# The last up pair of a ConvFFN in seven products, and the first operands of its down stage on freed bytes

## The chip, the cores and the metric

The kernel runs on one core of one Trainium2 chip. The metric is the device time of one execution in microseconds. A core has TensorE for matrix products (PE in the profile), VectorE (DVE), ScalarE (ACT), GpSimd (POOL) and SyncE (SP), which only issues DMA transfers. Each engine has an instruction queue of its own, which it works off in order; engines wait for each other by semaphores.

## The reference

One layer of a streaming encoder on 1024 positions and 16 meta tokens, with 1024 channels. The change concerns its last part, a gated feed-forward block with a causal convolution of width 3, and a residual:

```python
def _conv_ffn(xn, w_up, conv_w, conv_b, w_down):
    seq_len = xn.shape[1]
    hid = xn @ w_up
    hp = jnp.pad(hid, ((0, 0), (CONV_WIDTH - 1, 0), (0, 0)))
    conv = conv_b + sum(hp[:, j:j + seq_len] * conv_w[j] for j in range(CONV_WIDTH))
    val, gate = jnp.split(conv, 2, axis=-1)
    return (jax.nn.silu(gate) * val) @ w_down
```

`hid` has 2 × 2816 columns, so there are 22 tiles of 128 gate columns and 22 of value columns. Behind the block stands a final RMS norm.

## The kernel before

**Precision.** Every float32 product is made of three TensorE products. An operand x is cast to a shorter form (hi, by ScalarE: "cast") and the rest x − hi is kept as lo (by VectorE or GpSimd: "split", `split_lo`, L137). Then hi·hi, hi·lo and lo·hi are added up in PSUM.

**Up.** Pair c is one tile of gate columns and one of value columns. Pairs 1, 2 and 21 are "plain" (`plain_steps`, L1338): 2 tiles × 3 pieces of about 343 positions × 8 steps over the channels × 3 = 144 matmuls, each piece followed by ScalarE (L1361, bias and first convolution weight) and two VectorE steps (L1363). Pairs 3 to 20 are "block pairs" (`block_pair`, L1486): gate and value, two halves of the channels and two halves of the positions make a 2 × 2 block product, which `seven` (L215) computes with seven block products instead of eight. These need sums of the weights (`combine`, L1451, GpSimd), casts (L1304) and splits of seven weight blocks, and sums of the positions (the tiles T, made once). Each of the seven products runs over 2 pieces of 258 and 256 positions, 4 steps and 3 matmuls: 168 matmuls. Evictions go to ScalarE (`S.copy`) and VectorE (`add`), and afterwards the convolution runs over whole rows of 1024 (L1501, L1503).

`glue` (L1311) ends both kinds: silu on ScalarE, the product with the value half (on GpSimd; on VectorE for pair 21), and the store to the scratch tensor `a_d` in DRAM (by SyncE; by ScalarE's queue for pair 21, L1320). For the pairs in `SUMMED` GpSimd makes four sums more, which are stored too.

**Down.** The 11 double tiles j of `a_d` are multiplied with `w_down`, again by seven products for a 2 × 2 block. They go in four groups, (8, 9), (7, 0, 1), (2, 3, 4), (5, 6, 10), and for each group the products p run in the order 0, 4, 1, 2, 5, 3, 6. I write (g, p) for product p of group g. `forms(p, j)` (L1561) loads a tile of weights (`wr`) and one of `a_d` (`ar`), makes the sums (GpSimd, L1570 to L1576), casts both (ScalarE, L1583) and splits both: on GpSimd for products 0, 4 and 5, on VectorE for the others. `product` (L1677 and on) runs, for four row tiles and every j of the group, three matmuls of 512 columns (L1697 to L1699); group 0 has 24 matmuls in a product, the others 36. It evicts by ScalarE (L1702, L1705) or adds on VectorE (L1707) into `u2` (four tiles, u20 to u23 in the program) and into the rows of the result, `hs`.

**What sets the order.** Operands lie in slots of four tiles (`ops`); a product's slots come free when its matmuls are done. `prepare` calls `forms` for as many products ahead as there are free slots. A scheduler then orders each engine's queue, and calls of `after(a, b)` add edges by hand. Before the change the first down operands lie in memory that is free once the tiles T are closed (`st_t.close()`), that is, once pair 20 has ended; pair 21 doesn't use T.

## Time and profile before

| | |
|---|---|
| median of 3 runs | 1427.16 us (1426.06 to 1427.6) |
| profiled execution | 1427.24 us |
| its span, from first to last instruction | 1425.5 us |
| mean granted TensorE clock | 0.998 |
| busy: TensorE, VectorE, GpSimd, ScalarE | 99%, 75%, 54%, 50% |

The profile shows one execution. A row of its timeline gives the start in us from the span's start, the duration in us, the engine, the line of the kernel, the operation, out<-in by the program's names, the shape, and in brackets how long the engine had waited and for whom. A row of a group gives the busy time of all, the mean of one in ns, and the idle time ahead of them with its releaser. A row of windows gives busy us and the number of instructions of each engine in a stretch of time, then the granted clock, the share of time that the DMA engines were busy, and GB/s.

### The profile page before, as it was taken

The numbers are of one execution on the slowest core, as the hardware profiler recorded it, in microseconds if no ns is written. First come the engines' busy times: TensorE is split into PE (matmuls) and PEld (weight loads), VectorE is DVE, ScalarE is ACT, GpSimd is POOL, SyncE is SP. The second block draws the span as 40 slices with busy tenths as digits, with TensorE's granted clock in tenths as the row PEclk, the third lists the DMA queues.
The fourth block names the chain that finished last, engine by engine and source line by source line (L and its number), as shares of the span: only waits on it lengthen the run. The fifth ranks groups of instructions, "written<-read, shape, count | busy, mean of one in ns | idle before, by whom it ended". The sixth has DMA issues, their size and how long they took to land.

```text
span 1425.5 us, 26319 instructions
## 1 busy us (share of the span) xinstructions
PE 1410.6 (99%) x9607; PEld 1336.1 (94%) x9607; DVE 1070.3 (75%) x2048; ACT 709.0 (50%) x1381; POOL 764.2 (54%) x872
## 2 busy tenths in 40 slices
PE   8999999999999999999999999999999999999997
PEld 8999999988999999999889999999999999888886
DVE  7999889843667675655479977788886776788867
ACT  7647575423555555534546444344444345644444
POOL 1542257642466556326771334545555545888795
PEclk9999999999999999999999999999999999999999
DMA  8685644530156531087953246666753327864443
GB/s 298 176 203 147 160 106 133 172 119 31 53 156 161 127 111 57 23 287 267 216 161 124 73 114 183 183 173 177 178 142 113 98 79 258 327 205 133 129 94 118
DMA packets 93318, 216.17 MB, mean 152 GB/s; under 512 B 14802, under 2 KB 22610, under 8 KB 92804
## 3 DMA queue, kind: packets, MB, share of 16 engines
q1 hardware_dynamic: 74340, 170.28, 36.3%
q0 software_dynamic: 17696, 41.29, 15.1%
q10 hardware_dynamic: 1152, 2.91, 0.7%
q8 instruction: 76, 1.25, 0.4%
q14 instruction: 54, 0.44, 0.1%
HBM read 170.88 MB, written 71.71 MB: 170 GB/s over the span
## 4 chain that ended last, share of the span: by engine, by line
PE 95%; DMA 2%; issue 1%; ACT 1%; DVE 0%; POOL 0%; POOLq 0%; DVEq 0%; SPq 0%
PE mm L174 5%; PE mm L176 5%; PE mm L175 5%; PE sp L236 4%; PE sp L237 4%; PE sp L238 4%; PE tp L236 3%; PE tp L237 3%; PE tp L238 3%; PE mm L238 3%; PE mm L236 3%; PE mm L237 3%; PE po L966 3%; PE tp L920 2%; PE mm L1699 2%; PE mm L1698 2%
## 5 line engine op out<-in xcount | busy, mean ns | idle before, releaser
L174 PE MATMUL mm<-xhi,whi 128*128 128x342 f32 (+2 forms) x480 | 156.1, 325 | 0.0
L175 PE MATMUL mm<-xlo,whi 128*128 128x342 f32 (+2 forms) x480 | 155.4, 324 | 0.0
L176 PE MATMUL mm<-xhi,wlo 128*128 128x342 f32 (+2 forms) x480 | 154.6, 322 | 0.5 <-DMA wlo<-in_w_g_dram 0.5
L1313 POOL TENSOR_TENSOR ov<-ov,og 128x1024 f32<-128x1024 f32 x21 | 50.8, 2421 | 119.7 <-ACT og L1312 117.4
L137 DVE TENSOR_TENSOR sw<-sf,sw 128x512 fp32r<-128x512 f32 x72 | 73.4, 1020 | 46.2 <-ACT sw L1304 45.1
L1304 ACT CAST sw<-sf 128x512 fp32r<-128x512 f32 x72 | 44.9, 624 | 108.9 <-POOL sf L1451 80.1
L176 PEld LDWEIGHTS mm<-xhi,wlo 128*128 128x128 f32 x480 | 90.4, 188 | 1.3 <-DMA wlo<-in_w_g_dram 0.8
L174 PEld LDWEIGHTS mm<-xhi,whi 128*128 128x128 f32 x480 | 90.4, 188 | 1.1 <-issue 0.6
L175 PEld LDWEIGHTS mm<-xlo,whi 128*128 128x128 f32 x480 | 90.4, 188 | 0.4
L1451 POOL TENSOR_TENSOR sf<-raw,sf 128x512 f32<-128x512 f32 x36 | 62.9, 1748 | 38.8 <-DVE sw L137 38.7
L1451 POOL TENSOR_TENSOR sf<-raw 128x512 f32<-128x512 f32 x36 | 49.1, 1363 | 60.0 <-ACT ov L1361 21.5
L238 PE MATMUL mm<-xhi,sw 128*128 128x258 f32 (+1 forms) x288 | 81.0, 281 | 0.0
L236 PE MATMUL mm<-xhi,sw 128*128 128x258 f32 (+1 forms) x288 | 80.8, 280 | 0.0
L237 PE MATMUL mm<-xlo,sw 128*128 128x258 f32 (+1 forms) x288 | 80.7, 280 | 0.0
L883 ACT ACTIVATE pt<-pt,mx 128x400 f32<-128x400 f32 (+5 forms) x72 | 53.1, 737 | 45.2 <-DVE mx L876 44.9
L1503 DVE SCALAR_TENSOR_TENSOR ov<-hv,cwt,ov 128x1024 f32<-128x1024 f32 x36 | 69.9, 1942 | 0.4 <-ACT ov L1501 0.4
L885 POOL TENSOR_SCALAR pt<-pt,mx 128x400 f32<-128x400 f32 (+5 forms) x72 | 51.8, 721 | 33.3 <-DVE mx L884 28.3
L1304 ACT CAST sw<-raw 128x512 fp32r<-128x512 f32 x70 | 43.0, 621 | 45.0 <-PE sp L238 23.1
L137 DVE TENSOR_TENSOR sw<-raw,sw 128x512 fp32r<-128x512 f32 x70 | 57.9, 831 | 4.3 <-ACT sw L1304 4.0
L137 DVE TENSOR_TENSOR tl<-tp,th 128x512 fp32r<-128x512 f32 (+1 forms) x80 | 50.7, 634 | 12.2 <-ACT th L923 11.6
L923 ACT CAST th<-tp 128x512 fp32r<-128x512 f32 (+1 forms) x80 | 43.4, 543 | 32.1 <-PE tp L920 22.7
L852 POOL CAST qz<-q 64x128 fp32r<-64x128 f32 (+1 forms) x72 | 20.2, 283 | 67.2 <-PE sp L871 65.7
(722 smaller groups left out, 5727.2 us busy)
## 6 DMA issues: line engine op xcount, KB each, us to landing
raw<-in_w_up_dram SPq DMA_DIRECT2D x44, 512.0 KB, 3.7
t_d<-in_w_dn_dram POOLq DMA_DIRECT2D x44, 256.0 KB, 6.9
wr<-t_d SPq DMA_DIRECT2D x44, 256.0 KB, 3.4
ar<-a_d SPq DMA_DIRECT2D x41, 256.0 KB, 5.3
a_d<-ov SPq DMA_DIRECT2D x18, 512.0 KB, 2.6
wr<-in_w_dn_dram SPq DMA_DIRECT2D x33, 256.0 KB, 3.8
t_d<-in_w_dn_dram SPq DMA_DIRECT2D x22, 256.0 KB, 4.3
t_d<-t_d SPq DMA_DIRECT2D x22, 256.0 KB, 4.7
```

The source lines that it names most:

```text
L137: return eng.tensor_tensor(out_, src, hi.bitcast(F), ALU.subtract)
L174: yield PE.matmul(ps, whi[:, i, :], ahi[:, i], start=(i == 0), stop=False)
L175: yield PE.matmul(ps, whi[:, i, :], alo[:, i], start=False, stop=False)
L176: yield PE.matmul(ps, wlo[:, i, :], ahi[:, i], start=False, stop=(i == k - 1))
L236: PE.matmul(ps, a[0][:, i], bh, start=(i == 0 and not joins), stop=False, skip_group_check=True)
L237: PE.matmul(ps, a[0][:, i], bl, start=False, stop=False, skip_group_check=True)
L238: PE.matmul(ps, a[1][:, i], bh, start=False, stop=(i == kh - 1), skip_group_check=True)
L883: ends[:] = rd, S.activation(pt[:n, :kc], pt[:n, :kc], AF.Exp, bias=low, scale=-1.0, accum_out=nm[:n, 0:1])
L885: sc_.append(GP.tensor_scalar(pt[:n, :kc], pt[:n, :kc], nm[:n, 1:2], 1.0, ALU.mult, ALU.mult))
L1304: S.copy(hi, src)
L1451: sums.append(GP.tensor_tensor(f_, a, b, op))
L1503: V.scalar_tensor_tensor(out=o, in0=h_[:, j:SEQ + j], scalar=cwc(j, m), in1=o, op0=ALU.mult, op1=ALU.add)
```

## The change

1. Pair 21 becomes a block pair. `block_pair` now ends with the seven products, and what follows (convolution, silu, product, store) is a function of its own, `conv_pair`, which for pair 21 stands behind `product(0, 0)`.
2. The first down operands no longer wait for the end of T. New memory (`down0`) holds the first buffers for `a_d` and weights; some slots are now quarters of `xhi` and `xlo`, the positions' own operands, which come free one after another as pair 21's seven products end. The forms of (0,0), (0,4), (0,1) and (0,2) are made ahead of `product(0, 0)`.
3. The store of pair 21 to `a_d` goes from ScalarE's queue to GpSimd's.
4. Edges: casts of the first products stand ahead of the first eviction copies, the convolution of pair 21 behind those casts and splits, GpSimd's splits for (1,0) behind the splits of (0,5) and (0,3), the loads of `hs` ahead of those for (0,5).

```diff
     def glue(g_, v_, c):
-        S.activation(g_, g_, AF.Silu)
+        silu = S.activation(g_, g_, AF.Silu)
+        for cp_ in first_copy:
+            after(silu, cp_)
         (V if c == NFF - 1 else GP).tensor_tensor(v_, v_, g_, ALU.mult)
...
-        (S if c == NFF - 1 else SY).dma_start(rows, v_)
+        kept[c] = (GP if c == NFF - 1 else SY).dma_start(rows, v_)
...
+    down0 = pool(ctx, "down0", side="left")
+    for tag in ("a00", "w"):
+        down0.tile([P, 512], F, tag=tag, name="hold", bufs=2)
...
+        return hg, hv
+
+    def conv_pair(c, hg, hv, behind=()):
+        res = {}
+        halves = ((hg, NFF + c, "og"), (hv, c, "ov"))
+        for h_, m, tag in halves:
+            res[tag] = o = conv_out(m, tag)
+            act = S.activation(o, h_[:, :SEQ], AF.Identity, bias=cwc(3, m), scale=cwc(0, m))
+            if behind:
+                for hi in casts[4:8]:
+                    after(act, hi)
             for j in (1, 2):
-                V.scalar_tensor_tensor(out=o, in0=h_[:, j:SEQ + j], scalar=cwc(j, m), in1=o,
-                                       op0=ALU.mult, op1=ALU.add)
-            res.append(o)
-        glue(*res, c)
+                st_ = V.scalar_tensor_tensor(out=o, in0=h_[:, j:SEQ + j], scalar=cwc(j, m), in1=o,
+                                             op0=ALU.mult, op1=ALU.add)
+                for cut in behind[:4] if tag == "og" else behind:
+                    after(st_, cut)
+                if tag == "og":
+                    last_gate[:] = st_,
+        glue(res["og"], res["ov"], c)
...
     for c in range(3, NFF - 1):
-        block_pair(c)
-    st_t.close()
-    plain_pair(NFF - 1)
...
+        conv_pair(c, *block_pair(c))
...
+    def quarter(r, h_):
+        cols = slice((L - 512) * h_, (L - 512) * h_ + 512)
+        return [[t_[:, KH * r + 2 * q + w, cols] for w in range(2) for t_ in (xhi, xlo)] for q in range(2)]
+
+    ops = quarter(0, 1)
...
+            elif j in groups[1] and p == 0:
+                for cut_ in fifth + third:
+                    after(cut, cut_)
...
             if first and p == 0:
                 first_copy.append(S.copy(to, ps))
+                for hi in casts[:4 if len(first_copy) == 1 else 8]:
+                    after(first_copy[-1], hi)
...
                 first_add.append(V.tensor_tensor(to, to, ps, ALU.subtract if p in MINUS else ALU.add))
+                if first and p == 2 and t > 1:
+                    for cut in third:
+                        after(first_add[-1], cut)
+                if len(first_add) <= 4:
+                    after(first_add[-1], last_gate[0])
...
+    last_pair = block_pair(NFF - 1)
+    ready[0, 0] = [forms(0, j) for j in groups[0]]
+    st_t.close()
+    down1 = pool(ctx, "down1", side="left")
     dpool[0] = down1
-    for p in ORDER[:2]:
+    down1.tile([P, 512], F, tag="w", name="hold", bufs=6)
...
+    ops += small + quarter(0, 0) + quarter(1, 0)
+    for p in (4, 1, 2):
         ready[0, p] = [forms(p, j) for j in groups[0]]
+    after(kept[NFF - 2], first_loads[7])
+    for c in range(4):
+        h_load.append(SY.dma_start(hs[c], h_d[P * c:P * c + P]))
+        after(h_load[-1], first_loads[-1])
+    product(0, 0, ready[0, 0], True, False)
+    conv_pair(NFF - 1, *last_pair, behind=cuts)
     st_r.close()
```

What this makes of the queues is seen in the program's own order. On VectorE, before, the end of pair 21 stands directly behind its last convolution steps; `ov` is the value half, `og` the gate half:

```order
L1363 SCALAR_TENSOR_TENSOR ov_14620<-mm_14677,cwt_9030,ov_14620 128x340 [waits Activation_49]
L1363 SCALAR_TENSOR_TENSOR ov_14620<-mm_14677,cwt_9030,ov_14620 128x340 [waits DVE_49]
L1313 TENSOR_TENSOR ov_14620<-ov_14620,og_14527 128x1024 [waits DVE_49]
L1762 MEMSET eps_14756 128x1
L1707 TENSOR_TENSOR hs0_14762<-hs0_14762,mm_14792 128x512 [waits DMAHW0_49,DMAHW6_49,PE_49,Pool_49]
L1707 TENSOR_TENSOR hs1_14763<-hs1_14763,mm_14793 128x512 [waits DMAHW5_49,DMAHW7_49,DVE_49,PE_49]
```

In the changed program the same product, now L1317, stands here; the lines L1772 are additions of the down stage, into `hs` for (0,4) and into u20 and u21 for (0,2), and the last row is the first split for (0,3):

```order
L1772 TENSOR_TENSOR hs1_14777<-hs1_14777,mm_14837 128x512 [waits DMAHW2_49,PE_49]
L137 TENSOR_TENSOR xlo_98<-ar_14826,xhi_97 128x512 [waits DMAHW0_49,Activation_49]
L1518 SCALAR_TENSOR_TENSOR ov_14872<-hv_14559,cwt_9030,ov_14872 128x1024
L1772 TENSOR_TENSOR hs2_14778<-hs2_14778,mm_14838 128x512 [waits DMAHW3_49,PE_49]
L1772 TENSOR_TENSOR hs3_14779<-hs3_14779,po_14839 128x512 [waits DMAHW4_49,PE_49]
L1518 SCALAR_TENSOR_TENSOR ov_14872<-hv_14559,cwt_9030,ov_14872 128x1024 [waits DVE_49]
L1772 TENSOR_TENSOR u20_14780<-u20_14780,mm_15063 128x512 [waits PE_49]
L1772 TENSOR_TENSOR u21_14781<-u21_14781,mm_15064 128x512 [waits PE_49]
L1317 TENSOR_TENSOR ov_14872<-ov_14872,og_14868 128x1024 [waits DVE_49,Activation_49]
L137 TENSOR_TENSOR xlo_98<-ar_14945,xhi_97 128x512 [waits DMAHW2_49,Activation_49]
```

The product has moved behind all four additions of (0,4) and two of (0,2). On GpSimd, before, pair 20's product is followed by four splits of (0,5) (into `xlo`) and by the first split of (1,0):

```order
L137 TENSOR_TENSOR op3_14714<-ar_14741,op3_14714 128x512 [waits DMAHW7_49,Activation_49]
L1313 TENSOR_TENSOR ov_14511<-ov_14511,og_14507 128x1024 [waits Activation_49,Pool_49]
L137 TENSOR_TENSOR xlo_98<-ar_14870,xlo_98 128x512 [waits DMAHW1_49,PE_49,Activation_49]
L137 TENSOR_TENSOR xlo_98<-wr_14868,xlo_98 128x512 [waits DMAHW0_49,PE_49,Activation_49]
L137 TENSOR_TENSOR xlo_98<-ar_14878,xlo_98 128x512 [waits DMAHW3_49,PE_49,Activation_49]
L137 TENSOR_TENSOR xlo_98<-wr_14876,xlo_98 128x512 [waits DMAHW2_49,PE_49,Activation_49]
L137 TENSOR_TENSOR op1_14712<-ar_14916,op1_14712 128x512 [waits PE_49,DMAHW2_49,Activation_49,Pool_49]
```

In the changed program, after pair 20's product, come four splits for (0,4) (op0 and op1), the store of pair 21, four splits for (0,5) (op2 and op3), and the first split for (1,0):

```order
L1317 TENSOR_TENSOR ov_14518<-ov_14518,og_14514 128x1024 [waits DMAHW7_49,DMAHW2_49,Activation_49]
L137 TENSOR_TENSOR op0_14772<-wr_14784,op0_14772 128x512 [waits DMAHW4_49,Activation_49]
L137 TENSOR_TENSOR op0_14772<-ar_14786,op0_14772 128x512 [waits DMAHW5_49,Activation_49]
L137 TENSOR_TENSOR op1_14773<-wr_14792,op1_14773 128x512 [waits DMAHW6_49,Activation_49]
L137 TENSOR_TENSOR op1_14773<-ar_14794,op1_14773 128x512 [waits DMAHW7_49,Activation_49]
L1324 DMA a_d_81<-ov_14872 128x1024 [waits DMASW5_49,DVE_49]
L137 TENSOR_TENSOR op2_14893<-ar_14929,op2_14893 128x512 [waits DMAHW6_49,Activation_49]
L137 TENSOR_TENSOR op2_14893<-wr_14927,op2_14893 128x512 [waits DMAHW5_49,Activation_49]
L137 TENSOR_TENSOR op3_14894<-ar_14937,op3_14894 128x512 [waits PE_49,DMAHW0_49,Activation_49,Pool_49]
L137 TENSOR_TENSOR op3_14894<-wr_14935,op3_14894 128x512 [waits DMAHW7_49,Activation_49]
L137 TENSOR_TENSOR xlo_98<-wr_14991,xhi_97 128x512 [waits PE_49,DMAHW1_49,Activation_49,Pool_49]
```

The DMA row is new on this queue, and its wait on VectorE stands ahead of the splits for (0,5).

More of the change, by code (lines that the diff above doesn't have):

```diff
@@ L212, in to_feature @@
         return los
+    kept = {}
     def m_ps():
@@ L1442, in block_kernel @@
     PIECES = [(0, 258), (258, 256)]
+    down0 = pool(ctx, "down0", side="left")
+    for tag in ("a00", "w"):
+        down0.tile([P, 512], F, tag=tag, name="hold", bufs=2)
+    eps = down0.tile([P, 1], F, name="eps")
+    V.memset(eps, EPS)
     st_t = ExitStack()
     tq = pool(st_t, "tforms", side="left")
-    T = [[tq.tile([P, KH, NH], R, name=f"t{i}{w}") for w in "hl"] for i in range(4)]
+    T = {i: [tq.tile([P, KH, NH], R, name=f"t{i}{w}") for w in "hl"] for i in (1, 2, 0, 3)}
+    T = [T[i] for i in range(4)]
     sums = []
@@ L1512, in block_kernel, with weight_tile, raw_buffer, op_tiles @@
     for c in range(3, NFF - 1):
-        block_pair(c)
-    st_t.close()
-    plain_pair(NFF - 1)
-    down1 = pool(ctx, "down1", side="left")
-    small = [down1.tile([P, 4, 512], R, name=f"op{q}") for q in range(4)]
-    ops = [[t_[:, w] for w in range(4)] for t_ in small]
-    ops += featq
-    dpool = {}
+        conv_pair(c, *block_pair(c))
[3 more added lines that the diff above has]
+    ops = quarter(0, 1)
+    n_w = [0]
+    def weight_tile():
+        n_w[0] += 1
+        if n_w[0] % 8 in (1, 2):
+            return down0.tile([P, 512], F, tag="w", name="wr", bufs=2)
+        return down1.tile([P, 512], F, tag="w", name="wr", bufs=6)
+    def raw_buffer(j, tag):
+        pl = dpool[turn_of[j] % 4 // 2]
+        if pl is dpool[0] and tag == "a00":
+            pl = down0
+        return pl.tile([P, 512], F, tag=tag, name="ar", bufs=2)
+    def op_tiles(pl, q0, q1):
+        small = [pl.tile([P, 4, 512], R, name=f"op{q}") for q in range(q0, q1)]
+        return [[t_[:, w] for w in range(4)] for t_ in small]
+    dpool = {0: None}
     pairs = {}
@@ L1531, in raw_tile @@
         if (k, h_) not in pairs.setdefault(j, {}):
-            pairs[j][k, h_] = dpool[turn_of[j] % 4 // 2].tile([P, 512], F, tag=f"a{k}{h_}", name="ar", bufs=2)
+            pairs[j][k, h_] = raw_buffer(j, f"a{k}{h_}")
         return pairs[j][k, h_]
+    first_loads = []
     def behind(ld, j):
-        if h_load and j in groups[1]:
+        if h_load and len(first_loads) == 16:
             after(ld, h_load[-1])
+        if j in groups[1]:
+            after(ld, first_loads[-1])
+        if j in groups[0]:
+            after(ld, first_loads[-1] if first_loads else kept["raw"])
+            first_loads.append(ld)
     LAST = NFF // 2 - 1
@@ L1583, in forms @@
             hi = S.copy(slot[q], src)
+            if j in groups[0] and p == 0:
+                after(hi, kept["c1"])
+            elif j in groups[0]:
+                casts.append(hi)
+                if p in (3, 6):
+                    for hi_ in casts[12:16]:
+                        after(hi, hi_)
+            elif j in groups[1] and p == 0:
+                for hi_ in casts[12:20]:
+                    after(hi, hi_)
             if first_copy and j in groups[0] and p >= 5:
@@ L1588, in forms @@
                 cuts.append(cut)
+            if j in groups[0] and p == 6:
+                late_casts.append(hi)
+            elif j in groups[0] and p == 5:
+                fifth.append(cut)
+            elif j in groups[0] and p == 3:
+                third.append(cut)
+            elif j in groups[1] and p == 0:
+                for cut_ in fifth + third:
+                    after(cut, cut_)
             if first_add and eng is V and j in groups[0] and p > 2:
@@ L1593, in forms @@
         return slot
-    first_add, first_copy, cuts = [], [], []
+    first_add, cuts, late_casts, fifth, third, casts = [], [], [], [], [], []
     held = {}
@@ L1758, in block_kernel @@
     gfB = dn.tile([P, D], F, name="gfB")
-    dn.tile([P, 512], F, tag="a00", name="hold", bufs=2)
+    for tag in ("a00", "a01", "a10", "a11"):
+        dn.tile([P, 512], F, tag=tag, name="hold", bufs=2)
+    hs.update((c, dn.tile([P, D], F, name=f"hs{c}")) for c in (7, 6))
     sq = dn.tile([P, 512], BF, name="sq")
-    eps = dn.tile([P, 1], F, name="eps")
-    V.memset(eps, EPS)
-    u2 = [dn.tile([P, 512], F, name=f"u2{c}") for c in range(4)]
-    hs = [dn.tile([P, D], F, name=f"hs{c}") for c in range(4)]
-    hs += [dn.tile([P, D], F, name=f"hs{c}") for c in range(4, KD)]
-    small2 = [dn.tile([P, 4, 512], R, name=f"op{q}") for q in range(4, 6)]
-    ops += [[t_[:, w] for w in range(4)] for t_ in small2]
-    for c in range(4):
-        h_load.append(SY.dma_start(hs[c], h_d[P * c:P * c + P]))
-    for g, p in turns:
+    ops += op_tiles(dn, 2, 4) + quarter(1, 1) + op_tiles(dn, 4, 6)
+    hs.update((c, dn.tile([P, D], F, name=f"hs{c}")) for c in (4, 5))
+    cuts.clear()
+    ops += ready[0, 0]
+    for g, p in turns[1:]:
         prepare()
```

29 lines of the change are left out of this document (16 added, 13 removed).

## The prediction

> **What bounds the kernel now.** I read the page's busy shares first, then its chain of work, then windows and single rows around the place of the change.
>
> ```profile
> PE 1410.6 (99%) x9607; PEld 1336.1 (94%) x9607; DVE 1070.3 (75%) x2048; ACT 709.0 (50%) x1381; POOL 764.2 (54%) x872
> PE 95%; DMA 2%; issue 1%; ACT 1%; DVE 0%; POOL 0%; POOLq 0%; DVEq 0%; SPq 0%
> ```
>
> TensorE is busy for 99% of the span and is 95% of the chain. So only two things move the time: a change in the matmuls that TensorE must run, and a wait that it doesn't have now. The change has one of each kind, so I look at the stage by windows: the up pair 20 (a block pair), the up pair 21 (a plain pair), and three pieces of the down stage behind it.
>
> ```profile
> core 0: us, PE busy (x) PEld busy (x) DVE busy (x) ACT busy (x) POOL busy (x), PEclk, DMA share, GB/s
> 1163.97:1183.93 19.96, 19.96 (x170) 19.96 (x169) 11.85 (x19) 7.59 (x13) 6.81 (x5) 1.00 0.29 102
> 1183.93:1206.63 22.70, 22.70 (x146) 22.70 (x145) 13.91 (x19) 13.60 (x22) 15.69 (x9) 1.00 0.79 282
> 1206.63:1215.00 8.37, 8.37 (x39) 6.95 (x38) 5.31 (x9) 5.43 (x12) 0.00 (x0) 1.00 0.66 221
> 1215.00:1222.80 7.80, 7.80 (x36) 6.44 (x35) 3.04 (x5) 6.68 (x13) 5.06 (x4) 1.00 0.81 300
> 1222.80:1248.98 26.18, 26.18 (x117) 21.56 (x116) 24.71 (x28) 15.28 (x28) 25.51 (x16) 1.00 0.96 346
> ```
>
> In every one of them TensorE is busy throughout, at a granted clock of 1.00. GpSimd (POOL) changes from idle (0.00 in the third row) to full (25.51 of 26.18 us in the last): it is the second engine at the bound here, and VectorE (DVE) beside it, with 24.71, is the third. So a delay put on GpSimd's queue at the start of the down stage has no room to be made up before the next 26 us have passed.
>
> **The gain.** These rows of TensorE's timeline are the first matmul of pair 20, of pair 21 and of the down stage. I call the last D0.
>
> ```profile
> 1163.95 0.28 PE L236 MATMUL mm<-xhi,sw 128*128 128x258 f32 x1
> 1183.93 0.32 PE L1357 MATMUL mm<-xhi,sw 128*128 128x344 f32 x1
> 1206.63 0.40 PE L1697 MATMUL mm<-op 128*128 128x512 f32 x1
> ```
>
> A block pair takes 1183.93 − 1163.95 = 19.98 us for 7 products × 2 pieces × 4 × 3 = 168 matmuls (118.9 ns each), a plain pair 1206.63 − 1183.93 = 22.70 us for 144 (157.6 ns each). Pair 21 as a block pair saves **2.72 us**. Its operands need four sums more on GpSimd and seven splits instead of four.
>
> ```profile
> L1451 POOL TENSOR_TENSOR sf<-raw,sf 128x512 f32<-128x512 f32 x36 | 62.9, 1748 | 38.8 <-DVE sw L137 38.7
> L1451 POOL TENSOR_TENSOR sf<-raw 128x512 f32<-128x512 f32 x36 | 49.1, 1363 | 60.0 <-ACT ov L1361 21.5 <-DVE sw L137 19.6 <-DMA raw<-in_w_up_dram 13.1
> ```
>
> The sums are 2 × 1.75 + 2 × 1.36 = 6.2 us, made during pair 20, in whose window GpSimd had 6.81 of 19.96 us to do. I cost them at nothing; if that cover failed, each late sum would be worth up to 1.75 us.
>
> [...]
>
> **The moves that I cost at nothing.** The first down tiles now lie on bytes that are free before the last pair ends; casts, copies, conv and splits are given an order; the loads of h move ahead of those for the sixth product, called (0,5) here (group 0, product 5), and GpSimd's next splits, for (1,0), stand behind it. I followed the rows of the new order against the durations of this trace: the operands of (0,0), (0,4), (0,1) and (0,2) come ahead of their matmuls. (0,1) is the tightest.
>
> ```profile
> 1207.77 0.62 ACT L1583 CAST xhi<-ar 128x512 fp32r<-128x512 f32 x1
> 1208.29 0.62 ACT L1583 CAST xlo<-wr 128x512 fp32r<-128x512 f32 x1
> 1222.26 0.68 DVE L137 TENSOR_TENSOR xlo<-ar,xlo 128x512 fp32r<-128x512 f32 x1
> ```
>
> Its four casts, a step of 0.52 us each, now stand behind the first eviction of (0,0), from about D0 + 2.3 to 4.4, and VectorE's last split, 0.68, ends near D0 + 5.1; the first of its matmuls is number 30 of down (D0 + 6.8, at 227 ns each). That leaves some 2 us, and what is later than that adds in full. SyncE's queue is passed by the h loads and by pair 20's store; the DMA share was 0.66 to 0.81 there, so I give them nothing, and up to 1 us if they queue.
>
> **The wait that is added.** The last pair's store of a_d moves from ScalarE's queue to GpSimd's, ahead of the four splits for (0,5). GpSimd runs in order, so all behind the store waits for the product that it stores, which VectorE makes. On VectorE that product (ov·og, 1024 columns) now stands behind the second conv step and behind the adds into u20 and u21 of product (0,2).
>
> ```profile
> 1211.28 1.23 DVE L1313 TENSOR_TENSOR ov<-ov,og 128x1024 f32<-128x1024 f32 x1
> 1225.23 0.39 PE L1697 MATMUL tp<-xlo 128*128 128x512 f32 x1
> 1225.46 0.39 PE L1698 MATMUL tp<-xlo 128*128 128x512 f32 x1
> 1230.37 0.67 DVE L1707 TENSOR_TENSOR u<-u,mm 128x512 f32<-128x512 f32 x1
> 1230.97 0.67 DVE L1707 TENSOR_TENSOR hs<-hs,mm 128x512 f32<-128x512 f32 x1
> ```
>
> Before, the product began at 1211.28, D0 + 4.65. In the new order the add of u20 waits for the 83rd matmul of down and that of u21 for the 84th; these are, by number, the rows at 1225.23 and 1225.46 (D0 + 18.60 and 18.83), whatever product they belonged to before. So u20 starts at about D0 + 18.60 + 0.39 + 0.04 = 19.03, u21 0.60 later (the step between the two adds quoted), the product 0.60 after that, and it ends at 20.23 + 1.23 = D0 + 21.46. GpSimd, done with (0,4) long before, stands idle until then.
>
> Next the store's issue on GpSimd. No row of this kernel has that store there; two groups bound it.
>
> ```profile
> L511 POOL DMA_DIRECT2D g_d<-gs x21 | 11.6, 551 | 43.3 <-ACT gs L510 39.6 <-PE tp L2120 3.7
> L1709 POOL DMA_DIRECT2D hs<-h_d x4 | 4.6, 1284 | 0.0
> ```
>
> 0.55 to 1.28 us; I take the middle, 0.9, as neither is near to it in kind (one is a store, the other runs beside this stage's splits). GpSimd is free for (0,5) at **D0 + 22.36**.
>
> ```profile
> 1215.06 1.29 POOL L137 TENSOR_TENSOR xlo<-ar,xlo 128x512 fp32r<-128x512 f32 x1 [15.45 <-ACT xlo L1583]
> 1218.83 1.29 POOL L137 TENSOR_TENSOR xlo<-wr,xlo 128x512 fp32r<-128x512 f32 x1
> 1222.81 1.29 POOL L137 TENSOR_TENSOR op<-ar,op 128x512 fp32r<-128x512 f32 x1 [2.69 <-ACT op L1583]
> 1247.29 1.74 POOL L137 TENSOR_TENSOR xhi<-ar,xhi 128x512 fp32r<-128x512 f32 x1
> 1232.03 0.39 PE L1697 MATMUL po<-xhi 128*128 128x512 f32 x1
> 1255.06 0.39 PE L1697 MATMUL tp<-op 128*128 128x512 f32 x1
> ```
>
> A split takes 1.29 us while VectorE is idle and 1.74 beside its splits. Before, the four splits of (0,5) ran from 1215.06 to 1220.12, in good time. Now they end between 22.36 + 4 × 1.27 = 27.4 and 22.36 + 4 × 1.74 = D0 + 29.3; the last is wanted by matmul number 112 (counted from 0), in the old trace 1232.03 = D0 + 25.40. I take 1.45 each, for VectorE's splits of (0,3) run beside their first half: 28.2, a **stall of 2.8 us** (2.0 to 3.9).
>
> Behind them come the 16 instructions that GpSimd had from 1222.81 to 1249.03, again as 16: twelve splits for (1,0) and (1,4) and four sums. The last belongs to (1,4) and is wanted by matmul 213, 1255.06 = D0 + 48.43 by the old trace. Before they took 25.51 us busy, 1.59 each, beside the same VectorE work; so they end at 28.2 + 25.5 = D0 + 53.7, 5.2 us late. The 2.8 us stall is part of that, not beside it: TensorE is by then 2.8 late itself, and waits 2.4 more. At 1.27 each all 20 end at 22.36 + 25.4 = D0 + 47.8, no second stall; at 1.74 each at D0 + 57.2, 8.7 late.
>
> Behind (1,4) GpSimd's next operands lay 8 us and more ahead of their matmuls by my walk through the old trace, and TensorE has itself become later by then; I give them nothing. The end of the kernel, after these, shifts with TensorE.
>
> **The sum**, against the profiled execution, 1427.24 us: −2.72 + 5.2 = +2.5, **1429.7 us**. The median of the runs shown is 1427.16, 0.08 below it, which is left as it is.
>
> **Rivals.**
> *The gain stays whole.* The store doesn't hold what stands behind it, or the change's order isn't the one that decides there. 1427.24 − 2.72 = 1424.5. For it: the four splits were done at 1220.12 and wanted no sooner than the row below, 4.4 us later. Against it: GpSimd's queue runs in its order in every stretch read. Chance 0.09; it ends near the lower edge of what counts as no change, so about half of it is faster.
>
> ```profile
> 1224.55 0.39 PE L1698 MATMUL sp<-xlo 128*128 128x512 f32 x1
> ```
>
> *Only (0,5) stalls.* GpSimd works at 1.3 us an instruction because VectorE, too, waits for the stalled TensorE. Stall 1.7 to 3.3, time 1426.2 to 1427.8. Against it is the mean of 1.59 above. Chance 0.18.
> *GpSimd and VectorE slow each other more: slower.* All 20 instructions at 1.74, and the store at 1.28: D0 + 21.46 + 1.28 + 34.8 = 57.5, 9.1 late, 1433.6. It decides for "slower" from a mean of 1.58 on, with 0.9 for the store: 22.36 + 20 × 1.58 = 54.0, 5.5 late, 1430.0. From 1247.29 on the old trace does run at 1.74, which speaks for it; the mean over the 26 us speaks against. Chance 0.15 above 1431.
> *They take turns.* [...] Chance 0.04. [...]
> *Another wait ahead of (0,5)*, at (0,1) for instance, 1 to 3 us on top: 1431 to 1433. Chance 0.04.
> *A block pair isn't shorter*, with both stalls: 1427.24 + 5.2 = 1432.4. Against it are the two windows above. Chance 0.01.
>
> **How the numbers follow.** The forecast has 0.49, spread over 1428.2 to 1431. From the median, 0.2% is 2.85 us, about what a measurement of this kernel can tell from no change: faster is under 1424.3, slower over 1430.0. The forecast splits at 1430.0 into about 0.27 same and 0.22 slower; with the rivals, slower is 0.22 + 0.15 + 0.04 + 0.04 + 0.01 = 0.46, faster 0.05, same 0.49. The range runs from 1426.0, which leaves out the whole gain, to 1433.6, GpSimd at 1.74 throughout.
>
> **What would show it.** Right: in the new profile GpSimd is idle from the end of (0,4)'s splits to about D0 + 21.5, released by VectorE's product, then issues one DMA; TensorE waits for GpSimd's splits once or twice, about 2.8 and 2.4 us, and nowhere else in the down stage; pair 21 takes 20 us. Wrong: GpSimd's splits for (0,5) begin before D0 + 15; TensorE's waits there name a DMA, ScalarE or VectorE; or a wait of more than 1 us stands ahead of (0,5) or behind (1,4).

## The result, and the profile after

The changed kernel takes **1442.85 us** (median of 4 runs, 1440.24 to 1444.65); the kernel before, in the runs beside it, 1427.38 us (1426.06 to 1427.68). The ratio is 1.0109 (95% interval 1.0088 to 1.0129): about 15 us slower, 9 us above the upper end of the predicted range, and above the time of every rival. The profiled run, 1444.55 us, is one of the two longer ones of the four (the others took 1440.24 and 1441.14).

The page of the changed kernel, its span 1442.7 us: busy time of the engines.

```profile
PE 1413.0 (98%) x9631; PEld 1335.3 (93%) x9631; DVE 1084.9 (75%) x2053; ACT 712.0 (49%) x1384; POOL 762.1 (53%) x877
```

The view of waits, TensorE's rows (us in total, times, longest). The second was there before, as 5.2; the first is new.

```profile
PE mm L1758 <- DVE xlo L137: 16.5, 1, 16.5
PE mm L357 <- ACT uh L415: 5.1, 1, 5.1
```

So one wait stands out, as long as nearly all that the span has grown by, and its releaser is VectorE, not GpSimd as forecast. Windows of pair 20, of pair 21, of the down stage up to the wait, of the wait, and of what follows:

```profile
1162.99:1182.95 19.96, 19.96 (x170) 19.96 (x169) 14.51 (x21) 8.11 (x14) 10.10 (x7) 1.00 0.23 90
1182.95:1203.00 20.05, 20.05 (x171) 20.05 (x170) 10.14 (x15) 8.29 (x15) 13.73 (x9) 1.00 0.48 153
1203.00:1225.66 22.66, 22.66 (x99) 18.16 (x98) 16.18 (x22) 18.08 (x32) 0.67 (x2) 1.00 0.81 306
1225.66:1242.13 16.47, 0.00 (x1) 0.00 (x0) 16.47 (x2) 4.56 (x8) 15.87 (x13) 0.62 0.54 176
1242.13:1245.00 2.87, 2.87 (x7) 2.29 (x8) 2.87 (x5) 0.28 (x1) 0.00 (x0) 0.50 0.61 188
```

Pair 21 takes 20.05 us. GpSimd does 0.67 us of work in the third row, as forecast. In the fourth TensorE does nothing, GpSimd works on its 13 instructions, and VectorE is "busy" for all 16.47 us with two instructions. Rows of VectorE's timeline there:

```profile
1223.45 1.22 DVE L1317 TENSOR_TENSOR ov<-ov,og 128x1024 f32<-128x1024 f32 x1
1224.59 0.68 DVE L137 TENSOR_TENSOR xlo<-ar,xhi 128x512 fp32r<-128x512 f32 x1
1225.19 16.89 DVE L137 TENSOR_TENSOR xlo<-wr,xhi 128x512 fp32r<-128x512 f32 x1
```

The product, the first split of (0,3), 0.68 us, and the second: the same instruction, 16.89 us long. GpSimd's timeline over the same time:

```profile
1224.97 0.63 POOL L1324 DMA_DIRECT2D a_d<-ov  x1 [24.00 <-DVE ov L1317]
1225.62 1.27 POOL L137 TENSOR_TENSOR op<-ar,op 128x512 fp32r<-128x512 f32 x1
...
1240.28 1.25 POOL L137 TENSOR_TENSOR op<-wr,op 128x512 fp32r<-128x512 f32 x1
```

GpSimd waited 24.00 us for the product, issued the DMA, and ran 13 instructions without a gap at 1.25 us each (beside an idle VectorE a split took 1.29 in the kernel before, at 1215.06), up to 1241.53. VectorE's split ends 0.55 us later, at 1242.08. The program orders two row tiles of (0,3) ahead of (0,5), so TensorE stands at their third matmul, which needs this split.

What TensorE did behind the wait:

```profile
1242.13 0.80 PE L1758 MATMUL mm<-xlo,xhi 128*128 128x512 f32 x1 [16.47 <-DVE xlo L137]
...
1246.57 0.43 PE L1757 MATMUL sp<-op 128*128 128x512 f32 x1
```

Ten matmuls from 1242.13 to 1246.57 take 4.44 us instead of 10 × 0.227 = 2.27, at a granted clock of 0.50 (last window above): 2.2 us more.

**The sum** of profiled spans, 1442.7 − 1425.5 = 17.2 us. The down stage begins at 1202.95 instead of D0 = 1206.63: −3.7 (0.96 of it because pair 20 starts earlier). From its first matmul to its last it takes 231.84 instead of 210.44: +21.4. Its end behind the last matmul is 0.4 shorter. Of the 21.4, 16.5 are the wait, 2.2 the half clock, and 2.7 are left. They are no wait: the 576 matmuls of down between number 312 and number 888 start here, first two rows before, last two after:

```profile
1277.51 0.39 PE L1697 MATMUL mm<-op 128*128 128x512 f32 x1
1407.87 0.27 PE L1697 MATMUL mm<-op 128*128 128x224 f32 x1
1293.56 0.40 PE L1757 MATMUL mm<-op 128*128 128x512 f32 x1
1425.49 0.27 PE L1757 MATMUL mm<-xhi 128*128 128x224 f32 x1
```

130.36 us became 131.93, 2.7 ns more for each matmul, in a stretch without a wait; over the stage's 942 matmuls that would be 2.6, as an estimate.

### The profile page after: what moved, and what is told of

Read it like the earlier page. It is cut to its first block, busy times and chain, and to the rows that moved or that the text cites. A ratio compares the mean times of both kernels' runs of the same rounds, so it can differ in the third digit from the quotient of the medians.

```text
span 1442.7 us, 26383 instructions
## 1 busy us (share of the span) xinstructions
PE 1413.0 (98%) x9631; PEld 1335.3 (93%) x9631; DVE 1084.9 (75%) x2053; ACT 712.0 (49%) x1384; POOL 762.1 (53%) x877
## 3 DMA queue, kind: packets, MB, share of 16 engines
q8 instruction: 76, 1.25, 0.4%
## 4 chain that ended last, share of the span: by engine, by line
PE 97%; DVE 2%; issue 0%; ACT 0%; DMA 0%; POOL 0%; POOLq 0%; DVEq 0%; SPq 0%
PE mm L174 6%; PE mm L175 6%; PE mm L176 5%; PE sp L238 5%; PE sp L239 5%; PE sp L240 4%; PE tp L238 3%; PE tp L239 3%; PE mm L240 3%; PE mm L238 3%; PE tp L240 3%; PE mm L239 3%; PE po L968 3%; PE tp L922 2%; PE mm L1758 2%; PE mm L1759 2%
## 5 line engine op out<-in xcount | busy, mean ns | idle before, releaser
L137 DVE TENSOR_TENSOR sw<-sf,sw 128x512 fp32r<-128x512 f32 x76 | 79.1, 1041 | 47.8 <-ACT sw L1306 47.7
L1317 POOL TENSOR_TENSOR ov<-ov,og 128x1024 f32<-128x1024 f32 x21 | 50.8, 2420 | 116.1 <-ACT og L1314 113.7
L240 PE MATMUL mm<-xhi,sw 128*128 128x256 f32 (+1 forms) x304 | 85.5, 281 | 0.0
L238 PE MATMUL mm<-xhi,sw 128*128 128x256 f32 (+1 forms) x304 | 85.3, 281 | 0.0
L239 PE MATMUL mm<-xlo,sw 128*128 128x256 f32 (+1 forms) x304 | 85.3, 280 | 0.0
L1306 ACT CAST sw<-raw 128x512 fp32r<-128x512 f32 x69 | 42.4, 621 | 43.9 <-PE sp L240 21.4
L238 PEld LDWEIGHTS mm<-xhi,sw 128*128 128x128 f32 x304 | 57.3, 188 | 0.0
```

The source lines that it names most:

```text
L137: return eng.tensor_tensor(out_, src, hi.bitcast(F), ALU.subtract)
L238: PE.matmul(ps, a[0][:, i], bh, start=(i == 0 and not joins), stop=False, skip_group_check=True)
L239: PE.matmul(ps, a[0][:, i], bl, start=False, stop=False, skip_group_check=True)
L240: PE.matmul(ps, a[1][:, i], bh, start=False, stop=(i == kh - 1), skip_group_check=True)
L1306: S.copy(hi, src)
```

## The experiments

Three questions: what holds the split; what else the change costs; and where 2.7 ns a matmul come from. E1 to e4 are edits of the changed kernel. All ratios are against the kernel before, run beside them.

### What holds VectorE's split

*Theory 1*: a run of ready instructions on GpSimd, piled up behind the late product. *Theory 2*: the DMA issue on GpSimd.

**e1**, the store on SyncE, which removes both the wait on GpSimd and the issue:

```diff
-        kept[c] = (GP if c == NFF - 1 else SY).dma_start(rows, v_)
+        kept[c] = SY.dma_start(rows, v_)
```

> Theory 1 (ready queue): in the changed kernel GpSimd, freed by the held store, ran 13 instructions with no pause, and VectorE's second split for (0,3), which reads two operands from SBUF as they do, got no turn until GpSimd paused: 16.9 us for a split of 0.68. Theory 2 (DMA issue): the store's issue on GpSimd's queue is what blocked the split that began 0.2 us behind it. Here the store goes to SyncE's queue, so neither the hold-up nor the issue is left. Both expect the wait of 16.5 us for (0,3) gone, GpSimd's splits for (0,5) at about 1215 to 1221 us, and 1424.5 to 1428.5 us: the gain of 2.7 us is kept, less up to 4 us if the loads for (1,0), which still wait for the last pair's product, come late. If something else held VectorE's split (its own operands), it stays above 1438.

1435.66 us (1434.85 to 1436.67), ratio 1.0063 (1.0051 to 1.0076). The 16.9 us split is gone, and 7.2 us with it, but the rest is far from the 1424.5 to 1428.5 that was expected. TensorE's new waits:

```profile
PE po L1757 <- DVE hs L1772: 1.9, 1, 1.9
PE mm L1758 <- DVE xlo L137: 1.8, 1, 1.8
PE tp L1757 <- DVE u L1772: 1.4, 1, 1.4
PE sp L1757 <- DVE u L1772: 0.8, 1, 0.8
```

5.9 us, all on VectorE: 1.8 for a split of (0,3), the rest for additions. The matmuls behind the first two ran at half clock, 0.43 us apart. So there is a second cost, which the long split had covered.

**e2**, the store back on ScalarE's queue:

```diff
-        kept[c] = (GP if c == NFF - 1 else SY).dma_start(rows, v_)
+        kept[c] = (S if c == NFF - 1 else SY).dma_start(rows, v_)
```

> The store goes back to ScalarE's queue, as in the kernel before. There it stands ahead of the casts for (0,5) and (0,3) and waits for VectorE's product until about 1224.6 us. Both theories expect those casts some 10 us late and a wait of TensorE for (0,3) of 3 to 6 us. Theory 1: the run of splits that GpSimd then starts takes VectorE's splits for (0,3) with it, and the wait is 10 us or more, 1435 us and above. Theory 2: no DMA issue on GpSimd, so VectorE's splits take 0.7 to 1.8 us and the time is 1427 to 1432.

1434.97 us (1434.59 to 1436.82), ratio 1.006 (1.0046 to 1.0073), between the forecasts of the two theories. No split over 1.8 us there, as theory 2 had it, and a wait of 3.2 us for ScalarE's casts, which stood behind the store. It doesn't tell e1's rest apart.

**e3**, theory 1 alone: the store on SyncE, and GpSimd's first split of (0,5) made to wait for the product:

```diff
+                if not fifth:
+                    behind_result(cut, kept["mult"])
```

> The store goes to SyncE's queue, but GpSimd's first split for (0,5) is made to wait for VectorE's product, as the store did. So the hold-up stays and the DMA issue on GpSimd goes. Theory 1: the same run without a pause, VectorE's split of 12 to 17 us, 1438 to 1445 us. Theory 2: no split above 2 us, TensorE waits under 4 us, 1426 to 1431 us.

1433.97 us (1433.83 to 1434.65), ratio 1.0052 (1.0036 to 1.0067), again between the two forecasts, with 6.2 us of waits in the down stage. GpSimd and VectorE, rows of the timeline (the first names a cast that had ended at 1215.24; VectorE's product ended at 1224.81):

```profile
1224.93 1.60 POOL L141 TENSOR_TENSOR op<-ar,op 128x512 fp32r<-128x512 f32 x1 [24.00 <-ACT op L1628]
1226.50 1.73 POOL L141 TENSOR_TENSOR op<-wr,op 128x512 fp32r<-128x512 f32 x1
1225.32 1.76 DVE L141 TENSOR_TENSOR xlo<-wr,xhi 128x512 fp32r<-128x512 f32 x1
```

The same 24.00 us of idle time, the same run, and the engines alternate, each at about 1.75 us. Theory 1 alone falls.

**e4**, theory 2 alone: the store stays on GpSimd, and the (0,5) splits wait for VectorE's last (0,3) split, so that no run stands behind the issue:

```diff
+                if len(third) == 4:
+                    for held_ in fifth:
+                        behind_result(held_, cut)
```

> The store stays on GpSimd's queue; the four splits for (0,5) behind it wait for VectorE's last split for (0,3). Theory 1: VectorE is alone for its four splits, each 0.7 us; TensorE waits under 1.5 us for (0,3) and 3 to 6 us for (0,5), and 1428 to 1434 us come out; VectorE's next splits, for (0,6), may be the ones that get no turn then. Theory 2: the split beside the DMA issue is still long, several us, and TensorE waits for it at (0,3).

1432.56 us (1432.03 to 1433.69), ratio 1.0041 (1.0028 to 1.0055), the fastest of these and within theory 1's 1428 to 1434, so that it is e3 that decides against theory 1.

```profile
1224.43 0.63 POOL L1328 DMA_DIRECT2D a_d<-ov  x1 [24.21 <-DVE ov L1321]
1224.64 0.68 DVE L141 TENSOR_TENSOR xlo<-wr,xhi 128x512 fp32r<-128x512 f32 x1
```

The split starts 0.21 us behind the start of the issue (in the changed kernel 0.22) and takes 0.68; GpSimd's first split begins only at 1226.62. Theory 2 alone falls too. *Theory 3* is left: the issue and a run of GpSimd directly behind it.

**m1**, a bench in the kernel's place, whose own computation is left out: GpSimd makes ten splits in a row, VectorE three, begun at several points of the run; five tries without a DMA issue ahead of the ten, seven with. It also runs streams of matmuls for the question on spacing (below: theory A, the places of the operands, that is, their start 32, 64 or 96 bytes on or hi and lo far apart; theory B, not the places).

> This kernel leaves the whole computation out and measures two things by themselves. First, TensorE's spacing in streams of 96 matmuls of 512 columns whose operands begin 0, 32, 64 and 96 bytes behind a 128-byte line, and two streams whose hi and lo parts lie in two tiles far apart, as in the changed kernel's quarters; the first stream is repeated at the end. Theory A (addresses): the streams at 32 and 96 bytes, or those with parts apart, are 2 to 4 ns slower than the 227 ns of the others. Theory B (not addresses): all within 1 ns. Second, ten splits in a row on GpSimd and three on VectorE that start 0, 1, 2, 3 and 8 short ScalarE steps (about 0.3 us each) behind the start of GpSimd's run, without and with a DMA issue on GpSimd's queue ahead of the run. Theory 1 (ready queue): without a DMA, VectorE's first split waits for the whole run when it arrives late, and gets its turn at the next boundary when it arrives with the first. Theory 3 (issue and run together, as the last runs suggest): the splits get no turn only behind a DMA issue, and then for the rest of the ten, up to 12 us.

Rows of three tries, the first without the issue, VectorE's split between GpSimd's rows:

```profile
235.60 1.26 POOL L146 TENSOR_TENSOR lob<-src,hib 128x512 fp32r<-128x512 f32 x1 [8.49 <-ACT ticks L136]
235.92 1.48 DVE L151 TENSOR_TENSOR dva<-src,hia 128x512 fp32r<-128x512 f32 x1 [18.47 <-ACT ticks L139]
...
346.98 0.57 POOL L142 DMA_DIRECT2D out_dram<-src  x1 [9.88 <-ACT ticks L136]
347.14 13.22 DVE L151 TENSOR_TENSOR dva<-src,hia 128x512 fp32r<-128x512 f32 x1 [8.89 <-ACT ticks L139]
...
358.55 1.25 POOL L146 TENSOR_TENSOR loa<-src,hia 128x512 fp32r<-128x512 f32 x1
...
416.81 0.57 POOL L142 DMA_DIRECT2D out_dram<-src  x1 [10.45 <-ACT ticks L136]
420.04 10.16 DVE L151 TENSOR_TENSOR dva<-src,hia 128x512 fp32r<-128x512 f32 x1 [11.92 <-ACT ticks L139]
```

Without the issue VectorE has its turn behind GpSimd's first split (that ends at 236.86, VectorE's at 237.40). With it, it stands until the tenth has ended (359.80, VectorE's at 360.36). One of VectorE's splits does so in all seven tries, even where it came 2.7 us behind the issue's end (last two rows), and none in the five without the issue. **Theory 3 is shown**: for such a run the issue ahead of it makes the difference. That nothing else can do the same isn't shown, and the kernel before has a case without an issue (last section). What in the engines does this, no run tells.

### What the rest costs

**e9** does the change's first part alone: the kernel before with pair 21 as a block pair, in the old place and order.

```diff
-    for c in range(3, NFF - 1):
+    for c in range(3, NFF):
         block_pair(c)
-    plain_pair(NFF - 1)
```

> The kernel before with the first part of the change alone: pair 21 as a block pair, nothing else. The down buffers are then free only when pair 21's products end. The gain of 2.7 us is kept, but the first loads (3.4 to 5.3 us to land), a cast (0.6) and a split (1.3) stand between pair 21 and (0,0), and the convolution ahead of them on two engines: TensorE waits 6 to 12 us, and 2 to 3 us more at half clock, 1433 to 1439 us.

1440.67 us (1439.86 to 1441.48), ratio 1.01 (1.0083 to 1.0117), above the 1433 to 1439 expected.

```profile
PE sp L1697 <- DVE xhi L137: 2.4, 1, 2.4
PE sp L1696 <- DVE u L1706: 2.4, 1, 2.4
PE sp L1696 <- ACT xhi L1582: 2.0, 1, 2.0
PE mm L1696 <- DVE hs L1706: 1.7, 1, 1.7
```

Down begins 3.0 us earlier (1203.63), but these waits and three shorter ones are 10.8 us, and half clock stands behind some (0.43 us from matmul to matmul behind those of 2.0 and 2.4 us). Matmuls 312 to 888, with the old slots, take 130.36 us as before (from 1291.68 to 1422.04). I read the waits as the end of a block pair, which leaves the convolution over whole rows to the down stage, where a plain pair had done it piece by piece. The change's other parts mend some of it (e1 is 5 us better).

**e10** is e1 with pair 21's product on GpSimd, which takes 1.22 us of work from VectorE:

```diff
-        (V if c == NFF - 1 else GP).tensor_tensor(v_, v_, g_, ALU.mult)
+        GP.tensor_tensor(v_, v_, g_, ALU.mult)
```

> As e1, with the last pair's product on GpSimd (2.4 us) and not on VectorE (1.2 us). VectorE's splits for (0,3) then begin about 1.2 us sooner; GpSimd makes the product at about 1221 to 1223.5 us, and the splits for (0,5) behind it run until 1229. If VectorE's lateness is what TensorE waits for in e1 (1.8 us and the half clock behind it), 2 to 4 us are gained, 1432 to 1434; if GpSimd's, the wait moves to (0,5) and the time stays at 1434 to 1437.

1432.94 us (1432.72 to 1433.82), ratio 1.0049 (1.0034 to 1.0063): 2.7 us better than e1, as expected (2.1 when each is taken against the kernel before beside it). But the profile doesn't show the reason that was expected. The waits in down add up to 5.3 us, only 0.6 less than in e1; the larger part is that no matmul behind them ran at half clock (0.23 us apart again behind the longest, 1.72 us). Besides, the store on SyncE's queue, and the loads behind it, come 3.1 us earlier (1223.68 instead of 1226.76). VectorE's load behind D0 is thus not shown as the cause.

**e6** orders the product ahead of the additions into u20 and u21 instead (on top of e5, below):

```diff
+                if first and p == 2:
+                    after(first_add[-1], kept["mult"])
```

> As e5, and VectorE makes the last pair's product ahead of the adds into u20 and u21. In e1 the loads for (1,0) stood behind that product, and TensorE lost some 6 us between matmuls 168 and 264 to late operands and adds. If the late product is the cause, it is 1.3 us earlier at 1221 to 1222 us, and later, with VectorE's conv steps (2.3 us each beside GpSimd's splits in e1), and 1 to 3 us come back: 1431 to 1434. If those waits come from GpSimd and VectorE sharing time, nothing changes: within 1 us of e5.

1435.87 us (1435.52 to 1437.98), ratio 1.007 (1.0058 to 1.0083), no better than e1, and 1.7 better than e5, which neither forecast had: TensorE's longest wait, 2.0 us, is now for an addition into `u2`. Here the order moved the wait.

### The spacing

**e5**: e1 with `eps` 64 bytes long instead of 4, so that what lies behind it starts elsewhere (theory A):

```diff
-    eps = down0.tile([P, 1], F, name="eps")
+    eps = down0.tile([P, 16], F, name="eps")[:, :1]
```

> As e1, with the small tile eps made 64 bytes wide, so that the operand slots behind it begin on 64-byte lines again. In all kernels of the new layout the 942 down matmuls are about 230.5 ns apart, before they were 227. Theory A (addresses): the 436 matmuls from op slots go back to about 227 ns, 1.1 to 1.5 us gained against e1 (1434.2 to 1434.6), and 3.6 us (1432) if the quarters of xhi and xlo follow. Theory B: 230.5 as before, 1435 to 1436.5.

1437.54 us (1435.71 to 1438.38), ratio 1.0077 (1.0063 to 1.0091): no gain, and above both forecasts. Down begins 2.6 us later than in e1 (1205.81), so the stage itself tells more: matmuls 312 to 888 take 132.35 us (from 1286.42 to 1418.77), in e1 131.92 (from 1285.28 to 1417.20). The 227 ns don't come back.

**e7**: the kernel before with 32 bytes ahead of its operands.

```diff
+    down1.tile([P, 8], F, name="shift")
```

> The kernel before, with all down buffers moved by 32 bytes. Theory A: the slots op0 to op3, which then begin 32 bytes off a 64-byte line, go from about 227 to 229.5 ns, op4 and op5 the other way; 0.3 to 0.7 us slower in all. If a shift of 32 bytes is what makes the whole stage 230.5 ns apart, about 3 us slower. Theory B: no change.

1426.84 us (1425.74 to 1429.31, 11 runs), ratio 1.0004 (0.9995 to 1.0013): the 3 us of a whole stage at 230.5 ns don't come. A small cost does: matmuls 312 to 888 start at 1276.86 and 1407.69, 130.83 us apart instead of 130.36, of the size that theory A gave. In m1 streams at 0, 32, 64 and 96 bytes, with all four operands moved alike, take 226.7 to 227.0 ns a matmul, and operands in rows of 1040 elements over two tiles 230.7. So a start that is common to all four costs 0.3 ns at most, theory B falls, and where the operands lie does matter. *Theory C*: hi and lo in two tiles cost it. *Theory D*: the distance between the four operands, where it is no multiple of 2 KB; a row of `xhi` or `xlo` has 1040 × 4 = 4160 bytes.

**m2**, a second bench, the computation left out: streams of 96 matmuls with operands at chosen distances, then waits of chosen lengths.

> The whole computation is left out. First, streams of 96 matmuls of 512 columns, in this order after a warm-up of 144 and a first stream: slot as one line of 2 KB tiles (227 ns in m1); four rows of one tile 4160 bytes apart; 2112 bytes apart; hi and lo in two tiles on 2 KB steps; the two operands in two tiles; the changed kernel's quarter exactly (two tiles, rows 4160 bytes apart), at column 0 and at column 528; one op slot with one quarter; two line slots; the first again. Theory C (two tiles): 231 ns wherever hi and lo lie in two tiles, also on 2 KB steps, and 227 for rows of one tile. Theory D (distance): 231 ns wherever the distance is no multiple of 2 KB, also in one tile. A mix of op slot and quarter comes half-way if the cost belongs to a matmul's own operands. Second, TensorE is made to wait 12 times, 0.7 to about 3 us, ahead of 60 matmuls each: if the halved clock of the last runs belongs to the length of a wait, the first matmuls behind waits of 1.8 us and more run 427 ns apart for 3 to 4 us, and behind shorter ones 227.

First matmuls of streams that follow one another: 2 KB steps in one tile; 4160 bytes, one tile; 2112 bytes, one tile; hi and lo in two tiles, 2 KB steps in each; the two operands in two tiles, 2 KB steps in each; the kernel's `quarter`; a quarter's other column:

```profile
53.62 0.39 PE L110 MATMUL ps<-xhi 128*128 128x512 f32 x1
75.38 0.40 PE L110 MATMUL ps<-xhi 128*128 128x512 f32 x1
97.67 0.39 PE L110 MATMUL ps<-xhi 128*128 128x512 f32 x1
119.97 0.39 PE L110 MATMUL ps<-xhi 128*128 128x512 f32 x1
141.75 0.39 PE L110 MATMUL ps<-xlo,xhi 128*128 128x512 f32 x1
163.51 0.40 PE L110 MATMUL ps<-xhi 128*128 128x512 f32 x1
185.68 0.39 PE L110 MATMUL ps<-xhi 128*128 128x512 f32 x1
```

Each difference over 96: 226.7, 232.2, 232.3, 226.9, 226.7 and, for the quarter, 230.9 ns. Two tiles cost nothing, so theory C falls; rows 4160 or 2112 bytes apart cost 4 to 6 ns, and **of theory D that much is shown**. A multiple of 2 KB is not the condition: the two tiles of m2 lie one behind the other, 8 × 1040 × 4 = 33280 bytes apart, 512 over a multiple of 2 KB, and hi and lo at that distance took 226.9. Both dear distances are 64 bytes over a multiple of 2 KB. E7, dearer by 0.8 ns a matmul, moves some slots by 32 bytes against the others; no run varies such an offset alone. A stream with one op slot and one `quarter` ran at 232.7, dearer than the quarter alone and not half-way, so the slots cut well don't help their neighbours.

**e8**: e1 with each quarter in one tile, rows still 4160 bytes apart.

```diff
-        return [[t_[:, KH * r + 2 * q + w, cols] for w in range(2) for t_ in (xhi, xlo)] for q in range(2)]
+        return [[t_[:, KH * r + w, cols] for w in range(4)] for t_ in (xhi, xlo)]
```

> As e1, with the quarters' slots cut otherwise: a slot is four rows of xhi or four rows of xlo, where the changed kernel takes hi from xhi and lo from xlo. Theory C: the matmuls from quarters go from 230.3 to about 227 ns, 1.7 us gained against e1 (1434), and 3 us if those from op slots follow. Theory D: no change, 1435.7.

1437.86 us (1435.32 to 1438.68), ratio 1.0079 (1.0064 to 1.0094): no gain, as theory D has it. The total is 2.2 us above its forecast, but down begins 2.9 later than in e1 (1206.11); matmuls 312 to 888 take 132.33 us (from 1286.78 to 1419.11).

**e11**: e10 with other slots in the quarters' place from product (0,1) on, cut at 2 KB from `featq`, the kernel's flat view of the same tiles.

```diff
-    ops += ready[0, 0]
+    recut = {1: [featq[i] for i in (0, 1, 4, 5)], 2: [], 3: [featq[i] for i in (2, 3, 6, 7)]}
...
-        ops += ready[g, p]
+        ops += recut[p] if g == 0 and p in recut else ready[g, p]
```

> As e10, but a quarter of xhi and xlo is used as a slot once only, for group 0; afterwards the same bytes are cut as the kernel before cut them, four 2 KB steps in one tile. Theory D (distance): from matmul 168 on, spacing goes from 230.3 to about 227 ns, some 780 matmuls, 2.5 us gained against e10: 1430.4. If the streams of m2 don't carry over to the kernel: no change, 1432.9. A risk that is not the theory's: slots come free later, and GpSimd's splits for (1,0) may be late by a few us.

1435.83 us (1434.07 to 1437.15), ratio 1.007 (1.0057 to 1.0084), above both forecasts. A wait of 5.3 us for VectorE stands in group 1; that the slots come free later, the risk named ahead, is my reading of it.

**e12**: e11 with (0,2)'s splits on GpSimd.

```diff
-        eng = GP if p in (0, 4, 5) else V
+        eng = GP if p in (0, 4, 5) or p == 2 and j in groups[0] else V
```

> As e11, and the four splits for (0,2) go from VectorE to GpSimd, which is idle there. If what is left of the loss is VectorE's load ahead of (0,3) (two conv steps, eight adds and eight splits in 15 us), TensorE's waits for VectorE at (0,3) (1.7 us in e10) and behind (1.2, 1.3 and 0.8 us) shrink by half or more, 2 to 4 us gained against e11: 1426.5 to 1428.5. If GpSimd is the limit, the waits move to (0,5) and the time stays within 1 us of e11.

1433.3 us (1430.95 to 1435.43), ratio 1.0051 (1.0039 to 1.0064): 2.5 better than e11, short of the 1426.5 to 1428.5 expected. Its matmuls 312 and 888, then those of e10, whose slots are the quarters:

```profile
1280.50 0.39 PE L1757 MATMUL mm<-op 128*128 128x512 f32 x1
1411.48 0.26 PE L1757 MATMUL mm<-op 128*128 128x224 f32 x1
1281.36 0.40 PE L1757 MATMUL mm<-op 128*128 128x512 f32 x1
1413.29 0.27 PE L1757 MATMUL mm<-xhi 128*128 128x224 f32 x1
```

130.98 against 131.93 us: the new cut returns 0.95 of the 1.57 us, and comes near e7's 130.83, where op0 to op3 also start 32 bytes off the slots in `xhi` and `xlo`. Its waits, 2.9 and 1.4 us, are still VectorE's. No run was faster than the kernel before.

## Why the prediction was wrong, point by point

- **The gain: right.** Pair 21 takes 20.05 us instead of 22.70, 2.65 saved against 2.72. The rival that a block pair isn't shorter is out.
- **The wait that is added: its mechanism right, its price wrong.** GpSimd stood for 24.00 us and issued the DMA at 1224.97, D0 + 22.0 (21.46 forecast); the issue took 0.63 (0.9, range 0.55 to 1.28). The failing step is the next: "I take 1.45 each, for VectorE's splits of (0,3) run beside their first half". It shared out the slowing between the two engines by the rows of before. The 0.04 for *They take turns* rests on a term that no run shows: where the two engines did alternate, in e3, GpSimd's splits took 1.60 to 1.73 us and VectorE's 1.75 to 1.77. In the changed kernel GpSimd wasn't slowed at all, 1.25 us each, and VectorE's split stood for the whole run, 16.9 us. E3, e4 and m1 show that for this run it took the issue directly ahead, which the store's move to GpSimd made. Neither the 2.8 us stall nor the second, of 2.4, came: TensorE waited once, 16.5 us, for VectorE. One rival had a wait ahead of (0,5), but of 1 to 3 us and for no named engine; the list of what would make the prediction wrong had a wait that names VectorE.

Where no issue stands ahead, in m1, VectorE's split loses until the end of one split of GpSimd's (1.48 us in all). In the changed kernel it lost for thirteen instructions.

- **The price of a wait: missing.** The sum took a wait at its own length. The 16.5 us brought 2.2 more at half clock, and e1's waits of 1.84 and 1.87 us brought some too. In m2 a wait of 1.93 us is followed by seven steps of 0.43 us from matmul to matmul, one of 2.92 us by none. Under the row of each stand two windows of 3.41 us, the one in which the wait ends and the next; the second number is TensorE's busy time, the third from the end the granted clock:

```profile
321.29 0.50 PE L110 MATMUL ps<-xhi 128*128 128x512 f32 x1 [1.93 <-ACT ticks L138]
319.08:322.49 3.41, 1.49 (x7) 1.02 (x6) 1.68 (x5) 0.00 (x0) 1.00 0.00 0
322.49:325.90 3.41, 3.41 (x9) 2.66 (x9) 0.61 (x2) 0.00 (x0) 0.50 0.00 0
375.29 0.50 PE L110 MATMUL ps<-xhi 128*128 128x512 f32 x1 [2.92 <-ACT ticks L138]
373.69:377.10 3.41, 1.81 (x8) 1.51 (x9) 1.54 (x6) 0.00 (x0) 1.00 0.00 0
377.10:380.52 3.42, 3.42 (x17) 2.84 (x16) 1.64 (x3) 0.00 (x0) 1.00 0.02 5
```

The granted clock of m2 changed at 322.49, 325.90, 339.56, 342.97, 356.62 and so on, always whole steps of 3.41 us apart. In the changed kernel it changed at 1229.57 (1.00 to 0.50) and 1246.64 (back to 1.00), five such steps apart, but no whole number of steps from m2's (265.7 from the first, each counted from its span's start), so the grid lay elsewhere in that run. The wait of 1.93 us falls into one step, which is then idle for 1.92 of 3.41 us; the next step runs at half clock. The wait of 2.92 us is cut by a border into 1.32 and 1.60, and nothing follows. In m2 every step with 1.92 us and more of idle time was followed by half clock, and none at full clock with 1.68 or less; behind two steps that ran at half clock, with 1.08 and 1.44 us idle, the clock stayed at half. In the kernels e1's 1.75 us in a step brought it and e10's 1.72 didn't; one step of e2 with 1.87 didn't either. So in these runs the border for a step at full clock lies near half a step, and whether a wait of 1.8 to 3.3 us brought the half clock depended on where it fell, which is luck for the kernel: in m2 half clock stands behind waits of 1.93, 2.26 and 2.59 us, none behind 2.92 and 3.25, and again behind 3.58 to 4.58.

- **The moves costed at nothing: wrong, by some 10 us.** The step is the term "The moves that I cost at nothing", with at most 1 us for SyncE's queue. E1 has neither the hold nor the long split, so it is the rival *The gain stays whole*, for which the prediction had 1424.5 us; it takes 1435.66, 11.2 more. Its down stage begins 3.5 us earlier than before (1203.18), but takes 223.3 us from first to last matmul, 12.9 more. 5.9 of these are the waits, for VectorE each, 2.5 the spacing, and 4.5 are left for the matmuls directly behind the waits, thirteen of them 0.43 us apart. I had followed the operands of the products up to (0,2) against their matmuls, but neither those of (0,3) nor the additions, which free TensorE's PSUM tiles and queue on VectorE behind convolution, product and splits: 1.8 us of the waits are for a split of (0,3), 4.1 for additions. Three things make VectorE late in e1, and no run takes one away and leaves the others. The product stands in its queue. The pair's last two convolution steps take 2.31 and 2.37 us beside GpSimd's splits, which aren't held back any more; in the changed kernel 1.28 each. And SyncE's loads for group 1 stand behind the store of that product: six of them go out from 1216.52 on in the kernel before, two by 1218.70 in e1 and the next at 1227.17:

```profile
1216.52 2.94 SPq L1558 DMA_DIRECT2D ar<-a_d  x6
1227.17 3.40 SPq L1599 DMA_DIRECT2D ar<-a_d  x4
```

The addition that TensorE waits for at matmul 168 in e1 stands behind a split for whose cast VectorE had waited 2.77 us, and e4's one long wait, of 3.4 us, is for an eviction of ScalarE behind a cast that had waited 3.04 us for its load. E9, where the block pair alone, in the old place, costs 14.8, shows that the cost isn't that of the new places alone. The 4 to 5 us of waits in e10 and e12 were not put down to one cause.
- **The slots: missing.** That a slot's place could change a matmul's time was in no term. It costs some 2.6 us by the estimate above, nearly what the gain brings. M2 shows that two distances cost, e9 that the block pair itself doesn't, e12 that a better cut returns 0.95 of 1.57 us between the two matmuls. The rule behind it is open.
- **The net.** The changed kernel against e1 gives the long split its price in place: 1442.85 − 1435.66 = 7.2 us, and not 16.5. While VectorE stood, TensorE lost time that in e1 it loses in four shorter waits: these and the slow matmuls behind them are 10.4 us there, and 18.7 in the changed kernel.

## What to carry to other kernels

Before a DMA issue goes onto GpSimd's queue, look at what stands directly behind it: if that is a run of splits or sums, a split of VectorE may stand until the run ends (16.89 us here instead of 0.68), and the DMA belongs on another queue, or the run behind a wait. When pricing a moved step on a kernel whose TensorE is 99% busy, walk the evictions and the loads as well as the operands, and count with the half clock behind waits from about 1.8 us on (1.84 us in e1, then 0.43 us a matmul instead of 0.23), as something that may come and may not. When operands move to other bytes, keep the distances that they had: here rows 64 bytes over a multiple of 2 KB cost 4 to 6 ns a matmul.
